# A two-layer hybrid trunk whose instructions are listed by a planner in the kernel

## The chip, the core and the metric

The kernel runs on one core of a Trainium2 chip. Its engines work side by side, each through its own instructions in a fixed order: TensorE (PE; PEld is its weight load), VectorE (DVE), ScalarE (ACT), GpSimd (POOL), and SyncE (SP), which issues nearly all transfers. An engine that waits for a semaphore lets nothing behind that instruction pass. The metric is the device time of one execution in microseconds, the median of the runs shown. It is lower where the kernel is better.

## The reference

Two layers over 256 latent tokens and 256 context tokens of 2048 features. A layer is one input projection of 5648 columns, three branches over its columns, and one output projection.

```python
def hybrid_layer(h_lat, h_ctx, c, c_ctx, norm_g, w_mod, ...):
    shift, scale, gate = jnp.split(jax.nn.silu(c) @ w_mod + b_mod, 3, axis=-1)      # and the same of c_ctx
    z_lat = (rms_norm(h_lat, norm_g) * (1.0 + scale[:, None]) + shift[:, None]) @ w_in
    z_ctx = (rms_norm(h_ctx, norm_g) * (1.0 + scale_x) + shift_x) @ w_in
    ya = rglru_branch(...)     # both directions
    yb = gdn_branch(...)       # chunked gated DeltaNet, 4 heads, both directions
    yc = gqa_branch(...)       # 8 query heads, 2 key heads; latent tokens read both, context reads context
    mix_lat = jnp.concatenate([ya * silu(ga), yb * silu(gb), yc * silu(gc)], axis=-1) @ w_out
    h_lat = h_lat + gate[:, None] * mix_lat          # h_ctx likewise, not in the last layer

def rglru_scan(u, h0, w_r, b_r, w_i, b_i, lam):      # 8 blocks of 64 features
    ub = u.reshape(bsz, t_len, N_BLK_A, BLK_A)
    gate_r = jax.nn.sigmoid(jnp.einsum('btni,nij->btnj', ub, w_r).reshape(bsz, t_len, D_A) + b_r)
    gate_i = jax.nn.sigmoid(jnp.einsum('btni,nij->btnj', ub, w_i).reshape(bsz, t_len, D_A) + b_i)
    ...
```

The output is the latent tokens of the last layer after a final norm.

## The kernel before

Activations lie as [feature, token], 16 tiles `Y` of 128 features by 512 tokens (256 latent, 256 context). A projection goes by column tiles of 128 columns: 16 contraction steps of 128 features, each three float32r matmuls, since both operands are split into two parts (`wh`, `wl` of the weights, `xh`, `xl` of the activations; `accumulate`). The weights come as `wraw`; ScalarE makes `wh`, VectorE `wl`. A column tile collects in one of two PSUM banks `pz`.

**First stage of layer 0** (`start_layer`, `mod_narrow`). Shift and scale of layer 0 are needed before any projection. `mod_narrow` makes them one tile of 128 features after the other: eight chunks of weights (256 KB each) in 32 matmuls with 2 stationary columns and 128 moving ones into `pm`, at four column positions of the array side by side (`tile_position=(0, 32 * c)`), each two passes in float32. A transpose and three VectorE steps follow, then `modulate` makes `xh` and `xl` of that tile. Seven column tiles (`FIRST`) run along, step by step: at step k, 21 matmuls of 512 columns into `pz`, `pa`, `pb` and `pt`. `advance` puts one chunk of the next features' modulation between them, here and there two, so that a step has four visits of narrow products. Then come the columns of beta and alpha (`beta_alpha`, 32 rows out), and the other 37 column tiles one by one (`project`).

**Branches.** When a column tile is done, `consume` starts the branch work that it allows. That is a generator, a step of which runs between projection matmuls when a rough account of the engines' time (`Timed`, `Background.pump`) says that its operands should be there. In this text a *visit* is a stretch of branch or modulation matmuls between projection matmuls. Narrow visits use part of the array (the modulation, the 32 x 32 and 64 x 64 products of `invert`); full-width visits use all of it (transposes, attention, the recurrence of the heads).

**RG-LRU gates** (`rglru_scan`). Weights of two 64-feature blocks stand on the diagonal of a 128 x 128 matrix of zeros, for each gate, so that a gate of 128 features is three full-width matmuls of 512 columns (`product3`). There are 8 tiles and 2 directions, so 16 pairs of gates.

**Later modulation** (`mod_step`) comes in 128 chunks, mostly summed on VectorE (`macc`), six of them as narrow TensorE products (`wm`) between the layers, where the norm of layer 1 is made (`rms_bcast`).

The order on each engine is that in which the code emits, after the framework's scheduler has moved neighbours a little; `Timed` decides when a branch step is emitted.

## Time and profile before

| what | us |
|---|---|
| median of 3 runs | 1538.97 (1538.77 to 1541.72) |
| span of the profiled execution | 1537.5 |
| TensorE busy | 1477.6 |
| VectorE busy | 1173.4 |
| ScalarE busy | 739.5 |
| GpSimd busy | 112.9 |

TensorE's busy time is a union of modelled matmuls, which overlap one another; how fast it goes is read from the starts in the timeline, and what it waits from the idle time of a stretch. The span cut into stretches gives for each engine its busy time, then the granted TensorE clock, the mean busy share of the 16 DMA engines and the rate at which they moved data.

### The profile page before, as it was taken

How to read it: one execution, taken by the hardware profiler on the slowest of the kernel's cores; microseconds unless marked ns; L12 is line 12 of the kernel's file. 1: busy time of each engine (PE TensorE's matmuls, PEld its weight loads, DVE VectorE, ACT ScalarE, POOL GpSimd, SP SyncE). 2: the span in 40 equal slices, each digit the busy share in tenths (PEclk: the TensorE clock that was granted, in tenths of full speed). 3: DMA queues.
4: the chain of work that ended last, by engine and by line, in shares of the span. 5: the costliest groups of instructions: out<-in, count | busy, mean ns of one | idle time of the engine just before them, and what ended most of it. 6: DMA issues, size and time to landing. Idle time of an engine off the chain costs nothing.

```text
span 1537.5 us, 29960 instructions
## 1 busy us (share of the span) xinstructions
PE 1477.6 (96%) x11746; PEld 1200.2 (78%) x11746; DVE 1173.4 (76%) x2542; ACT 739.5 (48%) x1708; POOL 112.9 (7%) x114
## 2 busy tenths in 40 slices
PE   4999999999999999999999999999999999999996
PEld 2666768787877877788878887867977889779996
DVE  4444989898898898999748876787895676788755
ACT  3223445554444546655422224554644555677653
POOL 0000010100020010000011110010100100000011
PEclk9999999999999999999999998999999999999998
DMA  9996444343443463344436555544551333233553
GB/s 341 341 337 239 152 131 138 113 161 111 144 158 110 142 185 109 108 146 156 142 124 223 201 198 191 179 141 164 197 180 63 97 111 105 79 107 125 191 187 116
DMA packets 90686, 247.68 MB, mean 161 GB/s; under 512 B 9200, under 2 KB 20912, under 8 KB 90544
## 3 DMA queue, kind: packets, MB, share of 16 engines
q1 hardware_dynamic: 89392, 244.71, 47.7%
q8 instruction: 92, 1.51, 0.4%
q10 hardware_dynamic: 1152, 1.05, 0.2%
q14 instruction: 50, 0.41, 0.1%
HBM read 243.60 MB, written 2.13 MB: 160 GB/s over the span
## 4 chain that ended last, share of the span: by engine, by line
PE 80%; DVE 10%; DMA 4%; ACT 3%; issue 1%; POOL 1%; SPq 0%; DVEq 0%; POOLq 0%; ACTq 0%
PE pz L90 56%; PE pa L90 9%; PE pb L90 8%; PE pt L90 4%; PE pm L90 3%; DVE wb L90 2%; DVE wl L90 2%; DVE macc L90 1%; DVE th L90 1%; DMA wraw<-in_w_in 1%; DMA wa<-rows_d 1%; ACT wb L90 1%; DMA Y<-in_xT 1%; DVE u L90 1%; ACT t L90 1%
## 5 line engine op out<-in xcount | busy, mean ns | idle before, releaser
L90 PE MATMUL pz<-xh,wh 128*128 128x512 f32 (+1 forms) x1760 | 642.5, 367 | 1.7 <-ACT xh L90 1.7
L90 PE MATMUL pz<-xh,wl 128*128 128x512 f32 (+1 forms) x1760 | 629.9, 358 | 0.8 <-DVE wl L90 0.8
L90 PE MATMUL pz<-xl,wh 128*128 128x512 f32 (+1 forms) x1760 | 629.8, 358 | 0.0
L90 ACT CAST wh<-wraw 128x512 fp32r<-128x512 f32 x488 | 293.3, 612 | 335.8 <-PE pz L90 206.3
L90 DVE TENSOR_TENSOR wl<-wraw,wh 128x512 fp32r<-128x512 f32 x488 | 329.4, 683 | 135.7 <-ACT wh L90 133.4
L90 PEld LDWEIGHTS pz<-xl,wh 128*128 128x128 f32 x1760 | 331.8, 189 | 50.0 <-issue 3.1
L90 PEld LDWEIGHTS pz<-xh,wh 128*128 128x128 f32 x1760 | 331.9, 189 | 48.9 <-ACT xh L90 2.4
L90 PEld LDWEIGHTS pz<-xh,wl 128*128 128x128 f32 x1760 | 332.3, 189 | 42.4 <-DVE wl L90 1.2
L90 DVE SCALAR_TENSOR_TENSOR macc<-wm,cs,macc 128x512 f32<-128x512 f32 x400 | 293.3, 766 | 1.4 <-DMA wm<-in_w_mod 1.0
L90 PE MATMUL pb<-wb 128*128 128x128 f32 (+1 forms) x560 | 112.6, 328 | 3.6 <-ACT wb L90 1.9
L90 PEld LDWEIGHTS pb<-wb 128*128 128x128 f32 x560 | 79.6, 190 | 16.7 <-ACT wb L90 6.9
L90 POOL TENSOR_TENSOR o<-o,t 128x512 f32<-128x512 f32 (+1 forms) x28 | 30.5, 1091 | 326.2 <-ACT t L90 326.2
L90 ACT ACTIVATE wb<-pb,mx,rqa 128x512 f32<-128x512 f32 (+1 forms) x48 | 33.9, 707 | 42.6 <-DVE mx L90 42.3
L90 DVE SCALAR_TENSOR_TENSOR u<-zp,small,u 128x512 f32<-128x512 f32 (+1 forms) x72 | 50.6, 702 | 1.9 <-ACT u L90 1.7
L90 DVE COPY s<-pm 128x64 f32<-128x64 f32 x16 | 3.6, 225 | 62.5 <-PE pm L90 62.5
L90 ACT ACTIVATE xh<-u,modS 128x256 fp32r<-128x256 f32 x64 | 29.3, 502 | 45.1 <-DVE u L90 45.0
L90 ACT ACTIVATE t<-pt 128x128 f32<-128x128 f32 (+1 forms) x122 | 34.1, 280 | 32.0 <-PE pt L90 29.9
L90 PEld LDWEIGHTS pa<-c,s 32*32 32x32 f32 x2304 | 25.0, 107 | 21.7 <-issue 12.0
L90 ACT COPY s<-pm 128x128 f32<-128x128 f32 x16 | 4.3, 267 | 70.5 <-PE pm L90 70.5
L90 DVE TENSOR_REDUCE mx<-pb 128x1 f32<-128x512 f32 (+1 forms) x48 | 28.7, 599 | 10.3 <-PE pb L90 9.9
L90 POOL TENSOR_TENSOR rqa<-rqa,mhalf 128x4 f32<-128x4 f32 (+1 forms) x16 | 17.3, 1084 | 244.7 <-DVE rqa L90 244.7
L90 ACT COPY wb<-pb 128x512 f32<-128x512 f32 (+1 forms) x48 | 24.7, 515 | 21.7 <-PE pb L90 21.0
(259 smaller groups left out, 1812.7 us busy)
## 6 DMA issues: line engine op xcount, KB each, us to landing
wraw<-in_w_in SPq DMA_DIRECT2D x148, 512.0 KB, 3.6
wm<-in_w_mod SPq DMA_DIRECT2D x128, 512.0 KB, 3.6
wraw<-in_w_out SPq DMA_DIRECT2D x64, 512.0 KB, 4.2
wraw<-in_w_first SPq DMA_DIRECT2D x32, 448.0 KB, 4.6
wb<-in_w_mod SPq DMA_DIRECT2D x48, 256.0 KB, 5.6
kq<-in_w_mod SPq DMA_DIRECT2D x16, 512.0 KB, 5.1
Y<-in_xT SPq DMA_DIRECT2D x16, 256.0 KB, 5.3
wa<-in_w_mod SPq DMA_DIRECT2D x16, 256.0 KB, 5.7
```

Of the source, the lines that this page charges most:

```text
L90: return f(*args, **kw)
```

## The change

Every instruction now goes through `Planned`, which notes its engine, its operands and a cost from a formula in the instruction's size. `Plan.enter` finds what it depends on. At the end `Plan.order` plays the whole list through: `forward` gives each engine, when it is free, the most urgent ready unit; `backward` sets urgency from the end; after six rounds the list with the earliest modelled end is fixed, each instruction chained to the one before it on its engine. Units written under `plan.run()` stay together.

In the first stage a class `Narrow` takes the place of `mod_narrow`: one run of 32 narrow matmuls a step, loads three chunks ahead in three sets of buffers, and a matmul with 4 output columns in place of the transpose. The masks, rope tables and the weights of beta and alpha are loaded late. The gates' weights are packed without zeros, 64 rows to a gate and block, and the two blocks' products go to two row positions of the array and two PSUM banks.

```diff
+    def order(self):
...
+        for _ in range(PASSES):
+            end, lists, spans, freed = self.forward(unit, members, before, after, begins, urgency)
+            if best is None or end < best[0]:
+                best = (end, lists)
+            urgency = self.backward(end, spans, after, freed, data)
+        self.end, lists = best
+        for insts in lists.values():
+            for a, b in zip(insts, insts[1:]):
+                self.chain(ops[b][1], ops[a][1])
...
+                if e == "pe":
+                    if kind == "s" and mode != "s":
+                        cost += 0.095
+                    elif kind != "s" and mode == "s":
+                        cost += 0.21 if kind == "r" else 0.11
...
+            elif self.name == "dve":
+                tail = 0.085
...
+                cost = max(0.068 + n / (480 if op == "tensor_tensor_scan" else 1920 if fast else 960) + 0.06 * column, 0.06)
...
+        def run(self, u):
+            with plan.run():
+                for j in range(8):
+                    for c in range(4):
+                        pe.matmul(out=self.pm[32 * c:32 * c + 2, 0:P], lhsT=cs[:, 2 * j + c // 2, :], rhs=self.chunks[u][j][:, c * P:c * P + P],
+                                  start=(j == 0), stop=(j == 7), tile_position=(0, 32 * c))
+            self.mt = tmp("s", (P, P))
+            act.copy(out=self.mt, in_=self.pm[:, 0:P])
...
+        def end(self, u):
+
+            pe.matmul(out=self.pm[:, 0:4], lhsT=self.mt, rhs=sel4, start=True, stop=True)
+            dve.tensor_scalar(out=modA[0][:, u, :], in0=self.pm[:, 2:4], scalar1=self.one[:, u:u + 1], scalar2=sm[0][:, S_G + u:S_G + u + 1], op0=ALU.add, op1=ALU.mult)
+            dve.tensor_scalar(out=modS[0][:, u, :], in0=self.pm[:, 0:2], scalar1=sm[0][:, S_BM + u:S_BM + u + 1], scalar2=None, op0=ALU.add)
...
-                rg = split(rgt[:, T * d:T * d + T], rg[:, 0:T], rg[:, T:TT])
+                rg = split(rgt[:, P * d:P * d + P], rg[:, 0:P], rg[:, P:2 * P])
                 yield
                 a, gu = tmp("wb"), tmp("wb")
-                for g, dst in ((0, a), (1, gu)):
-                    pg = pb_()
-                    product3(pg, [x[:, P * g:P * g + P] for x in rg], us)
-                    act.activation(out=dst, in_=pg, func=AF.Tanh, scale=0.5, bias=hb[:, 8 * g + j:8 * g + j + 1])
-                    yield
+                pg = [pb_(), pb_()]
+                with plan.run():
+                    for i, (x, y) in enumerate(((0, 0), (1, 0), (0, 1))):
+                        for b, hf in enumerate(halves):
+                            pe.matmul(out=pg[b], lhsT=rg[x][hf], rhs=us[y][hf], start=(i == 0), stop=(i == 2), tile_position=(64 * b, 0))
+                for b, hf in enumerate(halves):
+                    act.activation(out=a[hf], in_=pg[b][hf], func=AF.Tanh, scale=0.5, bias=hb[hf, j:j + 1])
...
+                for b, hf in enumerate(halves):
+                    other = halves[1 - b]
+                    act.activation(out=gu[hf], in_=pg[b][other], func=AF.Tanh, scale=0.5, bias=hb[other, 8 + j:9 + j])
...
+        def late():
+            nonlocal bs
+            with plan.held():
+                late_loads()
+                rope_tables()
+                bs = gate_weights(0)
```

First place: TensorE in one contraction step of the first stage. The narrow products are those into `pm` from the chunks in `full`, `kq`, `wb`, `wa`, `th`; the others are projection matmuls. Before:

```order
L90 MATMUL pm<-full,cs 2x128 x8
L90 MATMUL pz<-xh_373,wh 128x512 x2
L90 MATMUL pa<-xh_373,wh 128x512 x2
L90 MATMUL pz<-xh_373,wl 128x512
L90 MATMUL pm<-kq,cs 2x128 x8
L90 MATMUL pz<-xl_374,wh 128x512
...
L90 MATMUL pm<-wb,cs 2x128 x8
L90 MATMUL pm<-wa,cs 2x128 x4
L90 MATMUL pa<-xl_374,wh 128x512
L90 MATMUL pm<-wb,cs 2x128 x4
```

Now, with `sel` as the four selecting columns:

```order
L381 MATMUL pz<-xl_608,wh 128x512
L381 MATMUL pz<-xh_607,wl 128x512
L381 MATMUL pa<-xh_607,wh 128x512
L381 MATMUL pm<-kq,cs 2x128 x16
L381 MATMUL pm<-wb,cs 2x128 x16
L381 MATMUL pz<-xl_608,wh 128x512
L381 MATMUL pa<-xh_607,wl 128x512
L381 MATMUL pa<-xh_607,wh 128x512
L381 MATMUL pm<-sel_121,s 128x4
L381 MATMUL pa<-xl_608,wh 128x512
```

The chunks that stood in four places of a step stand in one, and the product with `sel` follows a few matmuls behind.

Second place: TensorE at the border of the layers. `pt<-cst,o` and `pt<-cst,kv` sum the squares, `pt<-cst,r` spreads the norm, `wm` are chunks of later modulation. Before:

```order
L90 MATMUL pz<-xl_8186,wh 128x512
L90 MATMUL pm<-wm,cs 2x128 x16
L90 MATMUL pm<-macc,sel 2x128 x8
L90 MATMUL pt<-cst,t 128x128 x4
L90 MATMUL pm<-wm,cs 2x128 x7
L90 MATMUL pt<-cst,o 128x2
...
L90 MATMUL pm<-wm,cs 2x128 x17
L90 MATMUL pt<-cst,r_9688 128x128 x3
L90 MATMUL pm<-wm,cs 2x128 x8
...
L90 MATMUL pa<-xh_9760,wh 128x256
```

Now:

```order
L381 MATMUL pz<-xh_8180,wh 128x512
L381 MATMUL pz<-xh_8180,wl 128x512
L381 MATMUL pz<-xl_8181,wh 128x512
L381 MATMUL pt<-cst,kv 128x2
L381 MATMUL pt<-cst,o 128x2
...
L381 MATMUL pm<-macc,sel 2x128 x4
L381 MATMUL pt<-cst,kv 128x2
L381 MATMUL pt<-cst,r_9671 128x128 x4
L381 MATMUL pa<-xh_9743,wh 128x256 x2
```

The six chunks `wm` have moved up between the last output matmuls, and only the norm is left at the border.

Third place: TensorE at an RG-LRU gate pair (`pb<-wb` of 512 columns, six). Before:

```order
L90 MATMUL pz<-xl_1471,wh 128x512
L90 MATMUL pm<-macc,sel 2x128 x8
L90 MATMUL pa<-c,s 32x32 x16
L90 MATMUL pz<-xh_1562,wh 128x512
L90 MATMUL pz<-xh_1562,wl 128x512
L90 MATMUL pb<-wb 128x512 x2
L90 MATMUL pz<-xl_1563,wh 128x512
L90 MATMUL pb<-wb 128x512 x4
```

Now:

```order
L381 MATMUL pz<-xl_428,wh 128x512
L381 MATMUL pz<-xh_1056,wl 128x512
L381 MATMUL pz<-xh_518,wh 128x512
L381 MATMUL pb<-wb 128x512 x6
L381 MATMUL pz<-xh_518,wl 128x512
L381 MATMUL pz<-xl_1057,wh 128x512
L381 MATMUL pz<-xl_519,wh 128x512
```

Six matmuls stay together now; and the projection matmuls around them belong to two column tiles at a time (the numbers of `xh` run on in two sequences), where one column tile ran to its end before the next began.

## Rows read from the trace of the kernel before

**Rows 1.** The page: busy time, share of the span, instructions of each engine.
```profile
PE 1477.6 (96%) x11746; PEld 1200.2 (78%) x11746; DVE 1173.4 (76%) x2542; ACT 739.5 (48%) x1708; POOL 112.9 (7%) x114
```

**Rows 2.** Stretches: PE, PEld, DVE, ACT, POOL busy (count), clock, DMA share, GB/s.
```profile
0.00:32.25 32.25, 9.67 (x113) 7.54 (x113) 17.41 (x50) 14.24 (x27) 2.09 (x12) 1.00 0.94 336
32.25:157.50 125.25, 125.25 (x1288) 79.79 (x1288) 59.12 (x161) 34.66 (x80) 0.95 (x1) 0.99 0.87 304
157.50:1526.00 1368.50, 1341.98 (x10343) 1112.34 (x10341) 1090.14 (x2320) 690.57 (x1601) 105.59 (x96) 1.00 0.44 144
1526.00:1537.50 11.50, 0.71 (x4) 0.52 (x4) 6.71 (x14) 0.00 (x0) 4.26 (x5) 0.63 0.53 183
```

**Rows 3.** Timeline of TensorE in the first stage: start, duration, operation, count.
```profile
120.09 0.39 PE L90 MATMUL pb<-xh,wl 128*128 128x512 f32 x1
...
121.02 0.40 PE L90 MATMUL pb<-xl,wh 128*128 128x512 f32 x1
121.34 0.62 PE L90 MATMUL pm<-full,cs 128*2 128x128 f32 x16
...
124.84 0.40 PE L90 MATMUL pz<-xh,wl 128*128 128x512 f32 x1
125.08 0.27 PE L90 MATMUL pm<-cst,s 128*128 128x128 f32 x1
...
125.42 0.40 PE L90 MATMUL pa<-xh,wl 128*128 128x512 f32 x1
...
126.22 0.62 PE L90 MATMUL pm<-wb,cs 128*2 128x128 f32 x16
126.65 0.40 PE L90 MATMUL pm<-wa,cs 128*2 128x128 f32 x8
...
129.00 0.40 PE L90 MATMUL pb<-xl,wh 128*128 128x512 f32 x1
129.33 0.62 PE L90 MATMUL pm<-th,cs 128*2 128x128 f32 x16
...
130.22 0.39 PE L90 MATMUL pt<-xh,wl 128*128 128x512 f32 x1
```

**Rows 4.** Timeline of TensorE at the border of the layers.
```profile
926.36 0.40 PE L90 MATMUL pz<-xl,wh 128*128 128x512 f32 x1
...
930.17 0.37 PE L90 MATMUL pt<-cst,o 128*128 128x2 f32 x2
930.39 0.36 PE L90 MATMUL pt<-cst,kv 128*128 128x2 f32 x2
...
939.08 0.38 PE L90 MATMUL pa<-xh,wh 128*128 128x256 f32 x1 [0.36 <-ACT xh L90]
...
945.33 0.80 PE L90 MATMUL pa<-xh,wh 128*128 128x256 f32 x2 [2.05 <-ACT wh L90]
```

**Rows 5.** Stretches of the first stage, columns as in rows 2.
```profile
60.00:80.00 20.00, 20.00 (x231) 12.67 (x230) 9.72 (x30) 5.65 (x14) 0.00 (x0) 1.00 0.91 316
20.00:100.00 80.00, 75.81 (x827) 48.26 (x829) 36.64 (x112) 18.87 (x45) 1.05 (x1) 0.98 0.98 349
```

**Rows 6.** Timeline: a 64 x 64 run, a pair of gates.
```profile
241.44 0.68 PE L90 MATMUL pa<-full,c 64*64 64x64 f32 x16
242.05 1.16 PE L90 MATMUL pb<-wb 128*128 128x128 f32 x8
...
600.92 1.67 PE L90 MATMUL pb<-wb 128*128 128x512 f32 x6
...
602.15 1.27 ACT L90 ACTIVATE wb<-pb,hb 128x512 f32<-128x512 f32 x2 [0.77 <-PE pb L90]
```

**Rows 7.** Stretches behind the first stage, columns as in rows 2.
```profile
150.00:700.00 550.00, 540.13 (x4121) 426.74 (x4120) 489.88 (x1091) 281.82 (x714) 41.87 (x34) 1.00 0.42 136
...
905.00:950.00 45.00, 41.83 (x308) 32.88 (x307) 31.18 (x63) 14.46 (x30) 4.11 (x3) 0.89 0.61 206
950.00:1420.00 470.00, 457.79 (x4152) 389.68 (x4151) 358.11 (x826) 269.62 (x634) 32.16 (x33) 1.00 0.40 129
```

More of the change, by code (lines that the diff above doesn't have):

```diff
@@ L125, in trunk @@
     ct = big.tile([P, KT, 2], F32, name="ct")
-    nc.sync.dma_start(out=ct, in_=cT)
+    sync.dma_start(out=ct, in_=cT)
     cst = big.tile([P, C_END], F32, name="cst")
-    nc.sync.dma_start(out=cst[:, 0:C_TRI], in_=consts[:, 0:C_TRI])
+    sync.dma_start(out=cst[:, 0:C_TRI], in_=consts[:, 0:C_TRI])
+    sm = [big.tile([P, S_END], F32, name=f"small{l}") for l in range(2)]
+    sync.dma_start(out=sm[0], in_=small[0])
     ident = cst[:, C_ID:C_ID + P]
@@ L155, in trunk @@
         pool.memset(sel[:, m, m:m + 1], 1.0)
+    sel4 = big.tile([P, 4], F32, name="sel4")
+    for g in range(2):
+        dve.tensor_tensor(out=sel4[:, 2 * g:2 * g + 2], in0=ident[:, 32 * g:32 * g + 2], in1=ident[:, 64 + 32 * g:66 + 32 * g], op=ALU.add)
     tiny = big.tile([P, 1], F32, name="tiny")
@@ L289, in mod_chunk @@
         end = k + 2 == KT
-        for i in range(2):
+        if engine is pe:
+            with plan.run():
+                for i in range(2):
+                    mod_product(cs[:, k + i, :], wm[:, i], end and i == 1 and mod_state["acc"] is None)
+        for i in range(2 if engine is dve else 0):
             acc = mod_state["acc"]
-            if engine is pe:
-                mod_product(cs[:, k + i, :], wm[:, i], end and i == 1 and acc is None)
-            elif acc is None:
+            if acc is None:
                 acc = mod_state["acc"] = big.tile([P, 2, TT], F32, tag="macc", name="macc")
@@ L305, in mod_end @@
         if acc is not None:
-            for m in ms:
-                mod_product(sel[:, m], acc[:, m], m == ms[-1])
+            with plan.run():
+                for m in ms:
+                    mod_product(sel[:, m], acc[:, m], m == ms[-1])
         if q < 3:
@@ L364, in product3 @@
     def product3(out, a, b):
-        for i, (x, y) in enumerate(((0, 0), (1, 0), (0, 1))):
-            pe.matmul(out=out, lhsT=a[x], rhs=b[y], start=(i == 0), stop=(i == 2))
+        with plan.run():
+            for i, (x, y) in enumerate(((0, 0), (1, 0), (0, 1))):
+                pe.matmul(out=out, lhsT=a[x], rhs=b[y], start=(i == 0), stop=(i == 2))
     class Weights:
@@ L454, in transposes @@
         pt = pt or pt_()
-        for c in range(n):
-            pe.transpose(out=pt[:, c * w:c * w + w], in_=src(c), identity=ident[0:w, 0:w])
+        with plan.run():
+            for c in range(n):
+                pe.transpose(out=pt[:, c * w:c * w + w], in_=src(c), identity=ident[0:w, 0:w])
         return pt
```

530 lines of the change are left out of this document (424 added, 106 removed).

## The prediction

> **What bounds the kernel now.** I read the list of engines first, then the span cut into stretches, then the timeline where a stretch has slack. TensorE (PE) is busy 1477.6 of 1537.5 us [rows 1], so a gain must be PE work taken away or PE idle time closed. The four stretches [rows 2] tell where both are. Until 32.25 us PE mostly waits for input (9.67 us busy). From 32.25 to 157.50, layer 0's first stage, it is never idle. From 157.50 to 1526.00 it is idle 1368.50 - 1341.98 = 26.5 us, 2%. The last 11.5 us are the final norm and the output, in which PE does almost nothing. So ordering can win at most some 26 us in the long stretch; whatever more is won must come out of PE's own work.
>
> The first stage holds such work. In the timeline [rows 3] one contraction step lasts 129.33 - 121.34 = 7.99 us. Its 21 matmuls of 512 columns run at 0.233 us each (five starts from 120.09 to 121.02), 4.89 us. The step also has 64 passes of the narrow modulation products; sixteen take 126.65 - 126.22 = 0.43 us, 0.027 each, so 64 take 1.71. A switch between the two shapes is what costs: from 129.00 to 130.22 are 1.22 us, in which two 512-column starts (0.47) and sixteen narrow passes (0.43) leave 0.33 us for going in and out. A step has four such visits, 1.31 us. A full-width transpose between two matmuls costs only itself: 125.42 - 124.84 = 0.58 us for two starts and the transpose, 0.11 more than the two. Sum 4.89 + 1.71 + 1.31 + 0.11 = 8.02, against 7.99 measured.
>
> **The change, part by part.**
> *First stage in whole runs.* The order shows 61 visits of the narrow products ahead of the beta/alpha product before, 16 now: 45 x 0.33 = 14.9 us away. Added is a full-width product with 4 output columns in place of each transpose, two passes instead of one. The nearest row is the 2-column product of the norm, started every 930.39 - 930.17 = 0.22 us [rows 4]; 16 x (0.22 - 0.11) = 1.8 us back. A step becomes 4.89 + 1.71 + 0.33 + 0.22 = 7.15 us for PE. It needs 2.1 MB of modulation weights and 0.46 MB of projection weights, so 2.56 / 7.15 = 358 GB/s, and there the cover is thin: the DMA engines moved 349 GB/s between 20 and 100 us with a busy share of 0.98, and 316 in the worst 20 us of it [rows 5]. At 349 a step takes 7.3 us. From the other end: inputs, sixteen modulation chunks and sixteen weight chunks are 45 MB; 32.25 us at 336 GB/s bring 10.8 of them [rows 2], the other 34 take 98 us at 349 GB/s, so the last chunk is there at 130 and the stage ends some 11 us later (its run, the rest of step 14, step 15), at 141. PE alone, starting its first wide matmul at about 31 instead of 32.25 (tables and gate weights no longer stand ahead of the first chunk), would need 31 + 16 x 4.89 + 14 x 2.04 + 15 x 0.22 = 141 as well. Two limits this close don't overlap perfectly, and each wait for a chunk adds to PE's own time; I take an end at 145 against 157.50: **-12.5 us**, from 0 (DMA at 316 throughout, 8.1 us a step) to -16 (PE alone). The delayed loads (masks, rope tables, gate weights) queue on SP behind the last chunk, among the first weight tiles; the gate weights stand second there, and their product stands on PE behind the last step and six matmuls of the next tile, some 6 us of cover behind the last chunk's products.
>
> *RG-LRU gates in row tiles.* Now a pair of gates is six full-width matmuls of 512 columns [rows 6], 1.40 us at the pace of rows 3, and 16 such pairs 22.4 us. After, as many instructions use half the rows each, two beside each other. No row shows two row tiles in one column group side by side. Upper bound: they run one after the other, and 16 visits at 0.33 come on top, a loss of 5.3. Lower bound: exact halves, 11.2 + 5.3 = 16.5, a gain of 5.9. The nearest row is the 64 x 64 run: sixteen passes from 241.44 to 242.05, 0.61 us with the way in and out [rows 6], so (0.61 - 0.33) / 16 = 0.02 a pass, where a 128-column pass takes 0.11 [rows 3] and 64 columns in line would take half of that. So tiles of 64 rows do overlap there, though they differ in columns as well. I take **-6 us**. ScalarE pays: four half-partition reads in place of two, at 0.64 us each [rows 6], 32 x 0.64 = 20 us over 16 pairs. ScalarE is busy 690.57 of 1368.50 us in that stretch [rows 2], so it is covered, as long as PE has column tiles to run while the two gate banks stay held for 1.3 us longer.
> The Trainium skill (TensorEngine Tiling (Array Packing), PSUM Bottleneck) speaks against this part: tiling speeds up TensorE but not the emptying of PSUM, so that the copies may become the bound. By it the 20 us of ScalarE would come back on the path, if nothing covered them, and the gates would lose 14 us instead of gaining 6. ScalarE's share in the row above speaks for the cover, and I keep -6.
>
> *The planned order.* Same arithmetic, other order. On PE the full-width products of the branches stood in 282 visits behind the first stage and stand in 551 now, each with projection matmuls on both sides; narrow visits there go from 129 to 125, plus the 16 gate runs counted above. The transpose row says that a full-width visit whose operands are there costs nothing, so the splitting is free, and the narrow ones stay as dear as they were. What remains is waiting. Of the 26.5 us of idle time, 45.00 - 41.83 = 3.2 lie around the layer boundary and 9.9 and 12.2 in the two projections with their branches [rows 7]. The boundary costs more than its idle time: the last matmul of layer 0 starts at 926.36, the first of layer 1 at 939.08, and the second step stands still until 945.33, 2.05 us of that behind ScalarE's weight split [rows 4]. Now the six modulation chunks that filled the 12.7 us stand among the output matmuls instead: 96 passes at 0.027 are 2.6 us, and six visits up to 2 us. In the gap they cost up to twice that, at the lower clock (0.89 of full on average there [rows 7]), so that taking them out leaves 6 to 8 us of norm; I take 8. So 12.7 becomes 8 + 2.6 + 2 = 12.6: no gain there, but the stall at 945 should go since the weights come earlier: **-2.5 us**, bounds -6 and +3. In the rest, 22 us of idle time stand between chains of short steps on VectorE, ScalarE and GpSimd; VectorE is the fullest, 489.88 of 550 us from 150 to 700 [rows 7], and much of that is modulation sums that can wait. An order that knows durations can put those behind; one that is fixed can also be wrong by a step. From zero to all 22 us; I take half, **-11 us**. Waits shorter than a matmul's modelled end lie inside "busy" and could add a few us either way.
>
> Sum: -12.5 - 6 - 2.5 - 11 = -32. Span 1537.5 - 32 = 1505.5; the median of the runs is 1.5 us above this profile's span, so **1507 us**, 2.1% faster.
>
> **The rivals.**
> *Ordering wins nearly all* (chance 0.17): the 22 us and the boundary's 6 go, the first stage ends at PE's pace: -16 - 6 - 6 - 20 = -48, 1491 us. For it: the idle time is in few long waits of 1 to 2 us. Against: VectorE's 89% leaves little room.
> *Half of it* (0.16): one of the big terms fails, by the DMA (at 316 GB/s a step takes 8.1 us, no faster than now) or by row tiles that run in line. Then -20 or so, 1519 us. Within it, ScalarE's 20 us on the path have a chance of 0.03: PE would stand before the next product that needs a gate bank, 16 times 1.3 us, and the time would be 1527. That is the Trainium skill's rule named above (TensorEngine Tiling (Array Packing), PSUM Bottleneck).
> *The fixed order costs* (0.10): the planner sends the branches' products to PE the moment that its model has them ready, 551 + 141 visits between 157 and 1526. If an operand comes later than modelled, PE stands, since nothing behind may pass; before, fewer visits with a whole group behind each gave the other engines slack. Idle there is 26.5 us now. The other terms give 18.5 (first stage and gates), so it decides from 26.5 + 18.5 = 45 us of idle time, 0.065 us per visit; at 0.11 per visit there are 76 us, and the time is 1539 - 18.5 + 50 = 1570 us. Against it: the durations that the planner uses can be held against rows, and a visit costs nothing if its data are a matmul early.
> *It doesn't do what it says* is settled by the order: 16 whole runs stand there.
>
> **How the numbers follow.** Forecast 1507, own range 1496 to 1520, chance 0.55; the others as above, with 0.02 for an end below 1485. The range 1484 to 1534 takes in the fuller gain and the half gain and leaves out most of the slow case and the far end. Within 0.2% of now, which is about what a measurement of this kernel can tell from no change, ends little: 0.04. Faster 0.88, slower 0.08.
>
> **What would show it.** In the changed profile: the first weight tile after the first stage starts near 145 (over 150: DMA, and its share near 1 throughout; PE idle before the narrow runs); one step near 7.2 to 7.4 us; six gate matmuls in some 0.7 us plus 0.33; PE idle of about 13 us between there and the end of the last projection; a boundary gap of 8 us or so with PE's clock falling in it. I am wrong if PE's idle time grows past 45 us, or if six gate matmuls still take 1.4 us, or if a lone full-width visit with its data there costs more than its own 0.11 us per pass.

## The result, and the profile after

The changed kernel takes 1551.87 us (median of four runs, 1550.31 to 1553.57) against 1540.35 us before on the same chip: 1.0085 times as long, 95% interval 1.0062 to 1.0107. It is slower by 0.85%, where 1507 us were forecast. Its profiled execution spans 1548.4 us.

| place | before | after |
|---|---|---|
| end of the first stage (start of the beta/alpha product) | 159.60 | 148.76 |
| from there to the last projection matmul | 1364.1 | 1385.0 |
| six gate matmuls (before: at the pace of [rows 3]; after: first start to the next other matmul) | 1.40 | 0.90 |
| last matmul of layer 0 to the first of layer 1 | 12.72 | 9.38 |
| ScalarE's copies of the gates, in all | 21.4 | 43.8 |

So the three places that the change touches by hand (first stage, gate matmuls, layer boundary) became shorter, and more than that was lost in the rest behind the first stage. The copies are read from the groups of the page. The engine line of the page, which answers [rows 1]:

```profile
PE 1472.3 (95%) x11762; PEld 1203.0 (78%) x11762; DVE 1165.6 (75%) x2513; ACT 759.3 (49%) x1740; POOL 113.9 (7%) x114
```

The stretches (PE, PEld, DVE, ACT, POOL busy with counts, clock, DMA share, GB/s), which answer [rows 2]:

```profile
31.45:148.80 117.35, 114.51 (x1269) 87.37 (x1270) 54.91 (x133) 36.78 (x84) 0.95 (x1) 1.00 0.89 325
148.80:1536.00 1387.20, 1346.72 (x10336) 1106.21 (x10336) 1086.74 (x2321) 708.30 (x1632) 106.63 (x96) 1.00 0.44 141
```

TensorE (PE) does less work (1472.3 us busy instead of 1477.6), and is idle for 40.5 us in the long stretch instead of 26.5. Part of what it waits lies inside "busy" as well, as the prediction says of waits shorter than a matmul's modelled end. Where it stands now, from the groups of the page (busy, mean ns of one, idle time before them and its releaser), first of before, then of after:

```profile
L90 PE MATMUL pz<-xh,wh 128*128 128x512 f32 (+1 forms) x1760 | 642.5, 367 | 1.7 <-ACT xh L90 1.7
L90 PE MATMUL pz<-xh,wl 128*128 128x512 f32 (+1 forms) x1760 | 629.9, 358 | 0.8 <-DVE wl L90 0.8
```
```profile
L381 PE MATMUL pz<-xh,wh 128*128 128x512 f32 (+1 forms) x1760 | 579.0, 370 | 17.7 <-DVE t L381 5.8
L381 PE MATMUL pz<-xh,wl 128*128 128x512 f32 (+1 forms) x1760 | 574.6, 368 | 6.5 <-DVE wl L381 6.3
```

The projection matmuls, the work that runs while the branches wait for other engines, stood for 2.5 us before; now they stand for 24.2 us. The view of waits names what for (us in all, number of waits, the longest): weight splits (wl, wh), and PSUM banks of finished column tiles that VectorE has yet to empty (t, Y). The line of `pb` is a wait of the branches.

```profile
PE pz L381 <- DVE wl L381: 6.3, 8, 1.4
PE pz L381 <- DVE t L381: 5.8, 5, 2.3
PE pb L381 <- DVE wb L381: 5.4, 10, 1.2
PE pz L381 <- ACT wh L381: 2.8, 4, 2.0
PE pz L381 <- DVE Y L381: 2.8, 7, 0.8
```

One of those waits in the timeline (start, duration, operation; in brackets the idle time before it). The gate's ScalarE half (ACT t) is done at 541.93, and its VectorE half would free the bank. VectorE, in its fixed order, first runs five sums of a modulation, 3.40 us of filler, and two small steps; PE stands 2.28 us:

```profile
540.85 3.40 DVE L381 SCALAR_TENSOR_TENSOR macc<-wm,cs,macc 128x512 f32<-128x512 f32 x5
...
541.33 0.60 ACT L381 ACTIVATE t<-pz 128x512 f32<-128x512 f32 x1
...
542.72 0.39 PE L381 MATMUL pz<-xl,wh 128*128 128x512 f32 x1
544.16 0.48 DVE L381 TENSOR_SCALAR wa<-wa,bb 128x128 f32<-128x128 f32 x2
...
544.55 0.68 DVE L381 SCALAR_TENSOR_TENSOR t<-t,pz 128x512 f32<-128x512 f32 x1
...
545.38 0.49 PE L381 MATMUL pz<-xh,wh 128*128 128x512 f32 x1 [2.28 <-DVE t L381]
```

### The profile page after: what moved, and what is told of

It reads as the page before. It is cut to its first block, busy times and chain, and to the rows that moved or that the text cites. A ratio compares the mean times of both kernels' runs of the same rounds, so it can differ in the third digit from the quotient of the medians.

```text
span 1548.4 us, 30065 instructions
## 1 busy us (share of the span) xinstructions
PE 1472.3 (95%) x11762; PEld 1203.0 (78%) x11762; DVE 1165.6 (75%) x2513; ACT 759.3 (49%) x1740; POOL 113.9 (7%) x114
## 4 chain that ended last, share of the span: by engine, by line
PE 59%; DVE 19%; issue 9%; ACT 7%; DMA 4%; POOL 1%; SPq 0%; DVEq 0%; ACTq 0%; POOLq 0%
PE pz L381 43%; PE pa L381 7%; PE pb L381 5%; DVE macc L381 5%; DVE wl L381 4%; DMA wm<-in_w_mod 3%; PE pm L381 3%; ACT wb L381 2%; PE pt L381 2%; DVE wb L381 2%; DVE Y L381 1%; DMA wa<-rows_d 1%; DVE u L381 1%; ACT wh L381 1%; DVE t L381 1%
## 5 line engine op out<-in xcount | busy, mean ns | idle before, releaser
L381 PE MATMUL pz<-xh,wh 128*128 128x512 f32 (+1 forms) x1760 | 579.0, 370 | 17.7 <-DVE t L381 5.8
L381 PE MATMUL pz<-xh,wl 128*128 128x512 f32 (+1 forms) x1760 | 574.6, 368 | 6.5 <-DVE wl L381 6.3
L381 PE MATMUL pz<-xl,wh 128*128 128x512 f32 (+1 forms) x1760 | 570.6, 367 | 0.0
L381 PEld LDWEIGHTS pz<-xh,wh 128*128 128x128 f32 x1760 | 318.0, 189 | 76.9 <-issue 12.7
L381 PEld LDWEIGHTS pz<-xh,wl 128*128 128x128 f32 x1760 | 320.3, 189 | 57.6 <-DVE wl L381 12.3
L381 PEld LDWEIGHTS pz<-xl,wh 128*128 128x128 f32 x1760 | 319.3, 189 | 43.6 <-issue 2.5
L381 PE MATMUL pb<-wb 128*128 128x128 f32 (+3 forms) x560 | 113.4, 323 | 1.3 <-issue 0.7
L381 PEld LDWEIGHTS pb<-wb 128*128 128x128 f32 (+1 forms) x560 | 89.3, 188 | 18.4 <-ACT wb L381 2.8
L381 ACT ACTIVATE wb<-pb,mx,rqa 128x512 f32<-128x512 f32 (+1 forms) x48 | 33.9, 706 | 43.8 <-DVE mx L381 43.7
L381 ACT ACTIVATE wb<-pb,hb 64x512 f32<-64x512 f32 x64 | 43.8, 684 | 8.6 <-PE pb L381 6.5
L381 ACT ACTIVATE s<-pa,bb 128x128 f32<-128x128 f32 x96 | 32.1, 369 | 22.0 <-PE pa L381 21.8
```

The source lines that it names most:

```text
L381: inst = f(*args, **kw)
```

## Experiments

Each kernel is the changed one with the edit shown, unless another base is named. "Behind the first stage" is the time from the start of layer 0's beta/alpha product to the start of the last projection matmul in the kernel's own trace. The kernel before had medians of 1537.5 to 1540.4 us on these chips, so kernels that ran on different chips are compared by their ratio to it; 0.1% is 1.5 us. The mark between the two last columns is sharp to some 3 us only: besides the stage's own matmuls, up to 12 of the next column tile (0.233 us each) stand ahead of it, 9 before and 6 in the changed kernel. The sum of the two columns is free of that.

| kernel | gates | order behind the first stage | us | ratio (95%) | first stage ends | behind it |
|---|---|---|---|---|---|---|
| before | full | scheduler | 1540.35 | 1 | 159.6 | 1364.1 |
| changed | row tiles | planned | 1551.87 | 1.0085 (1.0062 to 1.0107) | 148.8 | 1385.0 |
| e3 | row tiles | scheduler | 1537.89 | 0.9996 (0.9983 to 1.0009) | 148.1 | 1371.4 |
| e5 | full | planned | 1546.94 | 1.0043 (1.0030 to 1.0056) | 147.7 | 1381.9 |
| e6 | full | scheduler | 1528.24 | 0.9921 (0.9896 to 0.9947) | 149.3 | 1362.8 |
| e10 | full, copies split | scheduler | 1540.86 | 1.0020 (1.0007 to 1.0032) | 148.9 | 1374.7 |
| e11 | row tiles, two copies | scheduler | 1529.23 | 0.9941 (0.9918 to 0.9963) | 148.1 | 1363.4 |
| e9 | full | planned, no lag | 1553.51 | 1.0104 (1.0078 to 1.0129) | 152.9 | 1383.5 |
| e16 | full | planned, no lag, slack | 1526.29 | 0.9903 (0.9883 to 0.9923) | 145.1 | 1364.2 |
| e18 | full | planned, lag, slack | 1527.48 | 0.9929 (0.9906 to 0.9951) | 143.1 | 1366.4 |

### The parts apart

*No planned order* (e1).
```
-    plan.order()
+    pass
```


> The changed kernel without its planned order: the last step of the planner (the call that sorts and chains all instructions) is left out, so the scheduler sets the order again as in the kernel before; the row tiles, the folded modulation and the runs of the first stage as written stay. Compiled, the projection matmuls change their PSUM bank 195 times (209 before, 4262 in the changed kernel) and the first stage has 47 narrow visits (61 before, 16 in the changed kernel). Theory A (the planned order puts two column tiles side by side, so that the projection matmuls, which hid every other wait, wait themselves for splits and banks): the idle time before the projection matmuls falls from 24 us back to about 3 us, and the time is 1540 less 4.7 us for the row tiles and less some 5 to 11 us for the first stage: 1524 to 1531 us. Theory B (the order is sound, what costs is the doubled ScalarE copies of the row tiles' gates, 22 us of work that now stand before the splits): the copies are still there, so the time stays at 1545 us or more. Theory C (the extra visits of the branches, 551 full-width ones instead of 282, cost by themselves): as theory A in time, since the visits go back to some 280, but with full-width visits dearer than 6 ns each in the changed kernel; told from A by the next run.

Measured: 1555.73 us, ratio 1.0103 (1.0072 to 1.0134). Theory A expected the cure; the time lies where theory B put it, at 1545 us or more. Without the plan the first stage has 47 narrow visits, starts its wide matmuls 3.8 us later (36.0 us) and ends at 161.4 us, so its gain needs the plan; and 1379.3 us follow behind it, 15 more than before, though the scheduler sets the order again. That left the row tiles as a cause, beside what the scheduler makes of this list.

*Planned order in the first stage alone* (e3). `upto` is the number of instructions written up to the end of that stage.
```
+                if a < self.upto and b < self.upto:
                     self.chain(ops[b][1], ops[a][1])
```


> The changed kernel with its planned order fixed for the first stage alone (the instructions written up to the end of layer 0's modulation and first seven column tiles); from there the scheduler sets the order as in the kernel before (233 changes of bank). The first stage is then instruction for instruction that of the changed kernel (16 narrow visits). Theory A: 1540 less 11 us (first stage) less 4.7 us (row tiles) = 1524 us (1520 to 1528), and the stage ends at 148 to 149 us. Theory B: the row tiles' copies cost after it, 1535 us or more.

Measured: 1537.89 us, ratio 0.9996 (0.9983 to 1.0009). The stage ends at 148.1 us as planned, 11.5 us early, and behind it 7.3 us are lost, 1371.4 against 1364.1, 6.6 of them in layer 1. Theory A's 1524 us held for the stage and failed for the gates. Theory B, ScalarE's copies, stood. The order has a part in it as well: behind the first stage e1 runs the same instructions under the same scheduler and takes 1379.3 us, 7.9 more, so the order that the scheduler happens to make is worth some 8 us by itself.

*Old gates*, with the planned order everywhere (e5) and in the first stage alone (e6).
```
-                pg = [pb_(), pb_()]
...
+                for g, dst in ((0, a), (1, gu)):
+                    pg = pb_()
+                    product3(pg, [x[:, P * g:P * g + P] for x in rg], us)
+                    act.activation(out=dst, in_=pg, func=AF.Tanh, ...)
```


> The changed kernel with the row tiles undone: the RG-LRU gates are again two products of three 128x128x512 matmuls per head and direction, each evacuated by one ScalarE copy of 128x512, with the old layout of their weights and bias; the planner orders everything as in the changed kernel. What is known from the first four runs: with the planned order fixed for the first stage alone the time is that of the kernel before (1538 us), although the first stage ends 11 us earlier; 13 us of that were lost in the RG-LRU stretches. Theory B (the row tiles cost: four ScalarE copies of 64 partitions, 684 ns each, in place of two of 128, some 1.4 us more in front of the weight splits for each of 16 pairs): without them the time falls to 1535 to 1543 us from 1552. Theory E (the row tiles save their 4.7 us as the PE rows say, and the planned order costs everything): 1555 to 1560 us.

> Planned order fixed for the first stage alone, the scheduler's order behind it, and the row tiles undone (old products of the gates): the first stage of the changed kernel beside everything else of the kernel before. Theory B (the row tiles cost some 12 us): 1525 to 1530 us, the best so far, with the 11 us of the first stage kept to the end. Theory E (the row tiles gain, the loss in the RG-LRU stretches of the run with them is the luck of the scheduler's order): 1536 us or more.

Measured: e5 1546.94 us (1.0043), e6 1528.24 us (0.9921). Undoing the row tiles gains 0.75% (11.5 us) under the scheduler's order and 0.42% (6.5 us) under the planned one. So theory B holds in direction in both, though e5 lies between the two ranges set for it (1535 to 1543 us for theory B, 1555 to 1560 for theory E). And e6 keeps the 11 us of the first stage to its end: behind it stand 1362.8 us, as before. The planned order behind the first stage costs by itself: 1.22% (18.8 us, e6 to e5) with full gates, 0.89% (13.7 us, e3 to the change) with row tiles. The changed kernel is thereby accounted for: first stage alone -12.2 us, planned order +18.8, row tiles +6.5, together +13.1, where 0.85% is +13.1. The three come from one chain of ratios and so add up by construction; each is known to some 4 us.

### What the row tiles cost

The rivals were the doubled copies, and the two banks held at once or the matmuls themselves. One run (e10) adds only the copies to e6, the other (e11) takes only the copies from e3; their edits in this order.
```
-                    act.activation(out=dst, in_=pg, ...)
+                    for hf in (slice(0, 64), slice(64, P)):
+                        act.activation(out=dst[hf], in_=pg[hf], ...)
```


> The best kernel so far (planned first stage, scheduler's order behind it, old gates; 1528.2 us) with each ScalarE copy of a gate split into two of 64 partitions by 512, so that ScalarE does the same four copies per head and direction as with the row tiles, while TensorE does the old six full matmuls. Theory B1 (the copies on ScalarE are what the row tiles cost): 1536 to 1544 us. Theory B2 (the copies hide, the cost lies in the two PSUM banks that the row tiles take at once, or in the matmuls): 1527 to 1532 us.


```
-                for b, hf in enumerate(halves):
-                    act.activation(out=a[hf], in_=pg[b][hf], ...)
...
+                for g, dst in ((0, a), (1, gu)):
+                    act.activation(out=dst, in_=pg[g], ...)
```


> Planned first stage, scheduler's order behind it, row tiles on TensorE as in the changed kernel, but each of their two PSUM banks evacuated by one copy of 128x512 straight to the place of the same partitions (this leaves the two gates mixed up in half of the channels; the work and the waits are otherwise the same). Theory B1 (the doubled copies are the cost): 1522 to 1529 us, against 1537.9 us with four copies. Theory B2 (banks or matmuls): 1534 to 1540 us.

Measured: the split copies alone take e6 from 0.9921 to 1.0020 (+15 us), and two copies instead of four take e3 from 0.9996 to 0.9941 (-8.5 us). The first is as theory B1 says, the second 0.2 us above its range of 1522 to 1529. (In e11 the two gates are mixed up in half of the channels, so it serves for the timing alone.) e11 keeps the two banks and the row-tile matmuls and lies with e6 within the noise, so the copies are the cause. With the changes from e5 to the changed kernel, e6 to e10 and e11 to e3, more copies made it slower three times; how much is less sure, since each time the order shifts too, and order alone was worth 8 us between e1 and e3. Nor does TensorE stand at the gates' banks. Its waits for the gate copies behind the first stage, and those for the weight split, in e3, then the first of them in e6:

```profile
PE pb L383 <- ACT wb L383: 1.8, 4, 0.7
...
PE pz L383 <- DVE wl L383: 6.1, 2, 5.0
```
```profile
PE pb L383 <- ACT wb L383: 1.9, 2, 1.4
```

The copies' groups (busy, mean ns), first of the changed kernel, then of e6:

```profile
L381 ACT ACTIVATE wb<-pb,hb 64x512 f32<-64x512 f32 x64 | 43.8, 684 | 8.6 <-PE pb L381 6.5 <-DVE th L381 0.9
```
```profile
L383 ACT ACTIVATE wb<-pb,hb 128x512 f32<-128x512 f32 x32 | 21.4, 683 | 12.2 <-PE pb L383 12.1
```

Half the partitions cost the same 0.68 us: splitting a copy by partitions doubles its time. And ScalarE has less room where the gates lie than over the span. The stretch of layer 1's gates, first before, then after, with the fullest 20 us of the changed kernel's (columns as above, ACT is the fourth busy number):

```profile
1325.00:1409.00 84.00, 80.65 (x817) 68.31 (x816) 68.02 (x142) 63.45 (x112) 0.71 (x1) 1.00 0.30 99
```
```profile
1325.00:1419.00 94.00, 89.11 (x919) 76.49 (x919) 75.52 (x158) 79.57 (x136) 0.00 (x0) 1.00 0.34 106
1375.00:1395.00 20.00, 17.32 (x160) 15.09 (x159) 15.05 (x29) 19.53 (x34) 0.00 (x0) 1.00 0.29 88
```

Over the whole span ScalarE is busy half of its time, in layer 1's stretch of the gates 85% (76% before), in the fullest 20 us 19.5 us. There PE stands for a weight split that is late on ScalarE:

```profile
1387.08 0.68 ACT L381 ACTIVATE wb<-pb,hb 64x512 f32<-64x512 f32 x1
...
1388.43 1.28 ACT L381 ACT_TABLE_LOAD   x1
...
1389.72 1.15 ACT L381 ACTIVATE th<-th,tiny 128x1024 f32<-128x1024 f32 x1
...
1390.89 1.28 ACT L381 ACT_TABLE_LOAD   x1
...
1392.46 1.13 ACT L381 CAST wh<-wraw 128x512 fp32r<-128x512 f32 x2
...
1393.13 0.90 PE L381 MATMUL pz<-xh,wh 128*128 128x256 f32 x2 [2.01 <-ACT wh L381]
```

The last copy ends at 1387.76. Right ahead of the split stand a step of RG-LRU and two loads of an activation table, which every kernel here makes alike (17 of them, 21.8 us); that the copies cost by pushing this row back is argued from ScalarE's order. How long the wait becomes depends on the order around it. In e3 (and in e1 at the same place) the RG-LRU chain came late to VectorE with the weight split behind it. The timeline of e3, and the stretches around it:

```profile
1375.02 0.40 PE L383 MATMUL pz<-xh,wh 128*128 128x256 f32 x2
1375.53 1.26 DVE L383 TENSOR_TENSOR_SCAN th<-wb 128x256 f32<-128x256 f32 x2
1376.71 1.37 DVE L383 TENSOR_TENSOR_SCAN th<-wb,th 128x256 f32<-128x256 f32 x2
...
1379.64 0.68 DVE L383 TENSOR_TENSOR wl<-wraw,wh 128x512 fp32r<-128x512 f32 x1
...
1380.38 0.58 PE L383 MATMUL pz<-xh,wl 128*128 128x256 f32 x1 [4.96 <-DVE wl L383]
```
```profile
1370.00:1375.00 5.00, 5.00 (x42) 4.84 (x42) 3.07 (x8) 4.97 (x9) 0.00 (x0) 1.00 0.00 0
1375.00:1380.00 5.00, 0.42 (x4) 0.21 (x2) 5.00 (x10) 0.86 (x2) 0.00 (x0) 0.84 0.00 0
1380.00:1385.00 5.00, 4.62 (x20) 4.49 (x21) 4.11 (x9) 2.35 (x5) 0.00 (x0) 0.50 0.58 192
```

PE stood 4.96 us and then ran at half clock (0.50, which is 1.2 GHz) for the next 5 us: 20 matmuls went where 42 of the same kind went in the 5 us ahead of the stall. So this stall cost some 7 us, about what e3 loses. In it ScalarE is busy for 0.86 of 5 us and VectorE for all 5: here the chain behind the copies is late, and not a copy itself.

### Why the planned order costs

Theory A came first: 4262 changes of PSUM bank in the planned order instead of 209 mean that two column tiles run side by side, so their weights and banks are wanted together.

*Projections in the order they are written* (e2; `in_row` is called after each projection matmul), and *one pass of the planner* instead of six (e4).
```
+    def in_row(self):
+        i = len(self.ops) - 1
+        if self.row is not None:
+            self.dep[i].add(self.row)
+        self.row = i
```


> The changed kernel with one rule more for its planner: each projection matmul comes after the one written before it, so that a column tile is finished before the next begins (276 changes of bank instead of 4262); everything else stays with the planner, which still makes 576 full-width visits to the branches. Theory A (two column tiles side by side make the projections wait): idle time before the projection matmuls falls by about 20 us and the time to about 1530 us (1525 to 1538). Theory B (ScalarE's gate copies) and theory C (the many visits): nothing changes, 1548 to 1556 us. Theory D (the planner's urgency puts the weight splits on VectorE and ScalarE too late, whatever the order on TensorE): the matmuls still wait for wl and wh, 1545 to 1560 us.


```
-PASSES = 6
+PASSES = 1
```


> The changed kernel with one pass of the planner instead of six: the order on each engine is made with the urgency of the order in which the program is written, without the passes from the end that reckon how late each step may be. Two column tiles still run side by side (3948 changes of bank). Theory A: idle time before the projection matmuls stays at some 20 us, time 1545 to 1558 us. Theory D (the urgency from the passes delays the splits): the projections no longer wait, 1525 to 1535 us.

Measured: e2 1653.63 us (1.0743), e4 1571.93 us (1.0210). The ranges of every theory were missed. In e2 column tiles are kept together and it is 100 us slower, which the planner's text explains (no run shows it by itself): a matmul that follows another counts as ready only 0.04 us after it, and in that moment any ready step of a branch goes first. The passes from the end are worth 19 us (1.0210 against 1.0085).

*No lag within an engine*, with row tiles (e8) and with old gates (e9).
```
-    done[j] if ops[j][0] != e else done[j] - ops[j][3])
+    done[j] if ops[j][0] != e else done[j] - ops[j][3] - 0.04)
```


> The changed kernel with one number taken out of its planner: as written, an instruction that continues another of the same engine (the next matmul into the same PSUM bank) counts as ready only 0.04 us after that one has ended, so at that moment the planner finds it not ready and takes something else that is: a matmul of the next column tile, or a step of a branch, however little urgent. Here it is ready at once. Compiled, the projections change their bank 197 times instead of 4262; row tiles stay. Theory G (this lag, not planning as such, makes the order that costs): PE's waits before projection matmuls fall, and the time comes to 1525 to 1540 us. If a fixed order costs whatever its rule is: 1548 to 1560 us. If keeping a column tile together costs, as the run with the projections in a row seemed to say: above 1600 us.

> The same planner without the lag, and the row tiles undone (old gates). Theory G together with theory B (the row tiles cost 5 to 10 us): 1515 to 1530 us, against 1546.9 us for the planned order with the lag and old gates, and 1528.2 us for the scheduler's order behind the first stage. If the lag is not the cause: 1543 to 1550 us.

Measured: e8 1559.18 us (1.0142), e9 1553.51 us (1.0104). With 197 changes of bank theory A's cause is gone, and the idle time before projection matmuls behind it falls, from 24.2 us in the changed kernel to 14.3 in e8 and from 16.5 in e5 to 6.6 in e9; yet the time is not better (e9 is even slightly above the range for "the lag is not the cause"). The waits of e9 behind its first stage show where they went, from the projections (pz) to the branches (pb, pa, pt):

```profile
PE pb L381 <- DVE wb L381: 12.3, 17, 2.5
PE pa L381 <- DVE o L381: 5.1, 5, 2.1
PE pt L381 <- DVE wb L381: 3.5, 1, 3.5
...
PE pz L381 <- DVE wl L381: 1.8, 2, 1.2
```

Theories A and G fall: side by side or one after the other, the stretch is about as long (1381.9 and 1383.5 us). What both plans share, by the planner's text, is that each step is put where its operands are ready by modelled time, with no room.

*Half a microsecond more on every result* (e7) was to test that.
```
-                done[i] = t + tail + 0.04
+                done[i] = t + tail + 0.5
```


> The changed kernel with one number of the planner changed: it reckons each result usable 0.5 us after the instruction's end instead of 0.04 us, so it leaves more room between a step and the steps that need it; row tiles as in the changed kernel; two column tiles still run side by side (4893 changes of bank). Theory F (the planned order is just in time by its own modelled times, and the real ones, which are longer, make TensorE wait): PE's idle time in the stretch from 150 to 1520 us falls from some 36 us and the time comes to 1535 to 1545 us. If the tight times are not the cause: 1548 to 1560 us.

Measured: 1789.65 us (1.1614). It tested something else: the next matmul into the same bank counts as late too, so the planner breaks every accumulation up (4893 changes of bank).

*The planned order on one engine at a time*, on e6: TensorE (e12), VectorE (e13), ScalarE (e14), SyncE and GpSimd (e15).
```
+                if a < self.upto and b < self.upto or ops[a][0] in ("pe",):
```


> Old gates, planned order fixed on all engines in the first stage (the base of 1528.2 us) and behind it on TensorE alone; VectorE, ScalarE, GpSimd and SyncE follow the scheduler. With all engines fixed the same plan took 1546.9 us, so the planned order behind the first stage costs 18.7 us. Theory P (the cost sits in TensorE's order, two column tiles side by side, 4269 changes of bank): 1540 us or more. Theory V (it sits in VectorE's, where long filler, the modulation's sums of 0.77 us each, is planned in a row ahead of what frees the PSUM banks): 1526 to 1534 us.

> The same base, with the planned order behind the first stage fixed on VectorE alone. Theory V (VectorE's planned order costs): 1540 us or more, with waits of TensorE for VectorE. Theory P (TensorE's): 1526 to 1534 us.

> The same base, with the planned order behind the first stage fixed on ScalarE alone. Theories P and V: 1526 to 1534 us. If ScalarE's order is what costs (splits of weights behind copies of the branches): 1538 us or more.

> The same base, with the planned order behind the first stage fixed on SyncE and GpSimd alone, so on the issue of the weight loads. Theories P and V: 1526 to 1532 us. Theory K (the planned order of the loads brings the modulation's chunks late, VectorE stands for them and all behind it): 1538 us or more, with VectorE idle before its sums.

Measured: 1681.72 (1.0926), 1633.23 (1.0615), 1591.62 (1.0353) and 1561.74 us (1.0158): each alone costs more than all together (1.0043). The orders of the engines belong together, so these four place nothing; they are inconclusive on the question.

*Slack for what another engine makes* (e16); the same with two modelled times brought to what the traces show (e17); slack with the lag kept (e18). All with old gates.
```
-    done[j] if ops[j][0] != e else done[j] - ops[j][3] - 0.04)
+    done[j] + 0.5 if ops[j][0] != e else done[j] - ops[j][3] - 0.04)
```


> Old gates, planned order on all engines, no lag between instructions of one engine (the run of 1553.5 us), and one number more in the planner: what another engine makes counts as usable 0.5 us later than the modelled end. The run with 0.5 us added everywhere (1789.7 us) had also held back the next instruction of the same engine, so it did not test this. Theory H (the plan is just in time by modelled times, and every real delay stops an engine that must keep its order): with slack the waits of TensorE fall and the time comes to 1525 to 1540 us. If slack is not what is missing: 1545 to 1560 us.

> The same with two modelled times brought to what the profile shows: a load of 256 KB or less lands 3.3 us instead of 0.9 us after its bytes have moved (the broadcast rows of the gated delta rule landed 5.6 us after their issue, the planner reckons 3.2 us), and GpSimd's power of 4 columns takes 1.3 us instead of 1.0. Theory H with theory M (the wrong times are what the fixed order stumbles on: GpSimd stood 31 us for those rows in the changed kernel against 11 us before, with the short steps behind it): a further fall of 5 us or more, to 1520 to 1535 us. If neither: as the run beside it.

> Old gates, planned order on all engines, the lag of 0.04 us between instructions of one engine kept as in the changed kernel (3836 changes of bank, two column tiles side by side), and the slack of 0.5 us for what another engine makes. It fills the fourth place beside 1546.9 us (lag, no slack), 1553.5 us (no lag, no slack) and 1526.3 us (no lag, slack). If slack alone is what the plan lacked: 1524 to 1532 us. If the side-by-side tiles cost by themselves once the branches have slack: 1537 to 1550 us.

Measured: e16 1526.29 us (0.9903), e17 1528.70 us (0.9924, 0.9903 to 0.9946), e18 1527.48 us (0.9929). One number takes 2.0% from e9 by the ratios; in the traces that is 27 us, 7.8 in the first stage (152.9 to 145.1) and 19.3 behind it (1383.5 to 1364.2). With the lag kept it takes 1.1% from e5. So slack is what the plan lacked in this kernel; whether two column tiles run side by side makes no difference that shows once it is there. Why it helps is argued from the planner's text and not shown: the slack also changes the order itself. Theory M is open. Right times on top gain nothing in all (e17), but its trace has 1360.0 us behind the first stage, 4.2 less than e16, and a first stage that ends 5.1 us later, since the edit makes the chunks of that stage count later as well. Late rows do not show in the time: the group in which GpSimd stands for the rows that the planner expects too early idles for 31.2 us in e16, 23.9 of them for the rows, against 31.3 for the rows in the changed kernel, which is 1.8% slower; and e18 is as fast as e16 with 55.7 us:

```profile
L381 POOL TENSOR_TENSOR wa<-wa,msk 128x512 f32<-128x512 f32 x16 | 20.1, 1264 | 31.2 <-DMA wa<-rows_d 23.9 <-DMA wm<-in_w_mod 4.9 <-DMA wraw<-in_w_in 1.2
```

e16 has the lowest time, 1.0% below the kernel before and 1.8% below the change, but e6, e17 and e18 are not told from it: their intervals overlap. Its stretch behind the first stage is as long as before (1364.2 us), so a plan with slack equals the scheduler's order there in sum (in layer 0 it takes some 6 us more than e6, in layer 1 some 5 less), and beats it only in the first stage.

## Why the prediction was wrong

**First stage, -12.5 us: right.** It ends 10.8 us earlier by the table's mark, 10.1 by the forecast's (157.50 was the start of the next column tile), and 12.2 us of the time stay when it is changed alone (e6). The timeline of one step, to hold against [rows 3]:

```profile
118.20 0.73 PE L381 MATMUL pz<-xh,wh 128*128 128x512 f32 x2
...
121.19 1.05 PE L381 MATMUL pm<-kq,cs 128*2 128x128 f32 x32
122.06 1.06 PE L381 MATMUL pm<-wb,cs 128*2 128x128 f32 x32
123.05 0.73 PE L381 MATMUL pb<-xh,wh 128*128 128x512 f32 x2
123.61 0.28 PE L381 MATMUL pm<-sel,s 128*128 128x4 f32 x2
...
125.73 0.72 PE L381 MATMUL pz<-xh,wh 128*128 128x512 f32 x2
...
133.49 0.73 PE L381 MATMUL pz<-xh,wh 128*128 128x512 f32 x2 [0.34 <-ACT xh L381]
```

One run of 64 passes takes 123.05 - 121.19 = 1.86 us, to which the ways in and out add some 0.1 each; 1.71 + 0.33 were reckoned. The step lasts 125.73 - 118.20 = 7.53 us against 7.15 to 7.3, the next one 7.76: PE waits at a step's start for the `xh` that ScalarE makes. With 0.5 us of slack in the plan that wait is nearly gone (PE idles 0.3 us in the stage in e16, 2.8 us in the changed kernel), and the stage ends at 145.07 us by the table's mark, some 142 by the forecast's, where 145 was forecast.

**Row tiles, -6 us: the sum for PE was right, the cover was not.** Six row-tile matmuls take 0.90 us, and 0.10 us each on the way in and out (the starts on either side are 0.33 us apart where the pace is 0.23), 1.10 against 1.40: 4.8 us in 16 pairs, where 6 were forecast. (The run in [rows 6] takes 1.50 us until the next matmul, 602.42 - 600.92; two of three run at the pace of 1.40.)

```profile
592.75 0.40 PE L381 MATMUL pz<-xh,wh 128*128 128x512 f32 x1
...
593.08 0.96 PE L381 MATMUL pb<-wb 64*128 64x512 f32 x6
...
593.98 0.50 PE L381 MATMUL pz<-xh,wl 128*128 128x512 f32 x1
594.08 2.11 ACT L381 ACTIVATE wb<-pb,hb 64x512 f32<-64x512 f32 x3 [1.44 <-PE pb L381]
```

The step that failed is "ScalarE is busy 690.57 of 1368.50 us in that stretch, so it is covered". That is an average over 1368 us; in layer 1's stretch of the gates ScalarE is busy 85% of the time with the copies, and 98% in the worst 20 us. The 20 us reckoned for the copies were 32 x 0.684 = 21.9, and the part came to +6.5 us in the planned order and +11.5 in the scheduler's, instead of -6. The prediction gave the case 0.03, and had its path off as well: PE does not stand at the gates' banks (1.8 us of waits in e3) but later, behind the weight splits. That the copies may become the bound is the rule of the Trainium skill (TensorEngine Tiling (Array Packing), PSUM Bottleneck), which was weighed there and set aside; the pair e10 and e11 agrees with the rule, with +15 and -8.5 us for the copies alone. Even with two copies the 4.8 us that PE saves don't arrive: e11 is not faster than e6, within the noise.

**Layer boundary, -2.5 us: right, and small.** From the last matmul of layer 0 to the first of layer 1 are 941.31 - 931.93 = 9.38 us instead of 12.72 [rows 4], and the wait of 2.05 us behind the weight split is gone.

```profile
931.93 0.40 PE L381 MATMUL pz<-xl,wh 128*128 128x512 f32 x1
...
938.11 2.08 PE L381 MATMUL pt<-cst,r 128*128 128x128 f32 x8 [1.35 <-POOL r L381]
941.31 0.80 PE L381 MATMUL pa<-xh,wh 128*128 128x256 f32 x2 [1.11 <-ACT xh L381]
```

**Planned order, -11 us: wrong in sign.** It costs 13.7 to 18.8 us. The rival *the fixed order costs* (0.10) names the mechanism, an operand that comes later than modelled while nothing behind may pass, and e16 and e18 fit it. Its place was off: the extra visits of the branches cost no more than before (with the matmul behind each, waits taken off, 306.2 us for 720 visits in e5 and 307.9 for 386 in e6), and the projections stood instead, until e9 moved the waits to the branches. Its threshold of 45 us of idle time was off too: 40.5 us were enough, since the gates' gain that it reckons with was a loss and part of the waits can't be seen as idle time. None of the three signs of being wrong that the prediction names for the changed profile came, and it was wrong all the same. In e5 the idle time behind the first stage is only 6 us longer than in e6, and "busy" 13 us longer for the same work: counted over the trace, away from the visits, 147 pairs of consecutive projection matmuls start 20 to 170 ns later than their pace in e5, 14.6 us in all, against 12 pairs and 1.3 us in e6. Waits so short fit inside a matmul's modelled end. That the waits could hide there was said and then given "a few us either way"; it was about twice the visible part.

The step that failed is "an order that knows durations can put those behind": it took half of the 22 us of idle time as a gain, from the idle time alone, without asking what room the order before leaves between a step and its use. With slack the plan is worth about nothing against the scheduler behind the first stage (1364.2, 1360.0 and 1366.4 us in e16, e17 and e18 against 1362.8 in e6, one trace each), and without it 14 to 19 us less than nothing.

Open: how the slack works, why 0.5 us is enough when single waits were 2 to 3 us long, and whether another value is better; one value was run. Slack with row tiles was not run.

## What to carry to other kernels

An order made from modelled times should ask for its cross-engine operands some time before they are due; here 0.5 us did, and without it rearranging the order only moved the waits to another place. A share of busy time says whether an engine covers more work only if it is read from the stretch in which that work falls. Before tiles by rows are used on TensorE, count the copies that empty their banks: here they doubled, since each bank held halves of both gates, while the matmuls went from 1.40 us to 1.10 with the ways in and out. And a change of several parts is worth running as its parts: here one part gained 12 us and the whole lost 13.

## What the runs showed of the hardware

A ScalarE copy of 64 x 512 from PSUM (tanh with a bias) took 684 ns, one of 128 x 512 683 ns. Two row tiles of 64 x 128 side by side took 0.15 us a matmul of 512 columns in the run of six, not the half of 0.233. A stand of 4.96 us was followed by 5 us at a granted clock of 0.50 in e3, in which 20 matmuls went where 42 had gone in 5 us at full clock. Projection matmuls kept the same pace of 0.233 us where two column tiles in two PSUM banks take turns (e5) and where one runs to its end (e6).
